# Attention of a hybrid encoder block: matmul pairs over halves of 64 array columns, values as the stationary side, probabilities normalised before they are split

## The chip, the cores and the metric

The kernel runs on one core of a Trainium2 chip. The metric is the time of one execution on the device in microseconds (us), as the median of several runs; lower is better. The engines are named as in the profile: PE is TensorE's matmuls and PEld its weight loads, DVE is VectorE, ACT is ScalarE, POOL is GpSimd, SP is SyncE, which here only issues DMAs.

## The reference

One encoder layer over 1024 tokens of width 1024, in float32. A combined projection gives queries, keys, values and gates of two groups of eight heads, 64 wide.

```python
h = jnp.einsum('bsd,de->bse', x, w_in[layer])
q_a, k_a, v_a, z_a, q_b, k_b, v_b, z_b = jnp.split(h, SPLIT_POINTS, axis=-1)
y_a = neighborhood_attention(q_a, k_a, v_a, rel_pos_bias[layer])   # heads of 64 split off
y_b = windowed_gqa_with_sink(rotary(q_b), rotary(k_b), v_b, sink_logits[layer])
mixed = jnp.concatenate([y_a * jax.nn.silu(z_a), y_b * jax.nn.silu(z_b)], axis=-1)
y = jnp.einsum('bse,ed->bsd', mixed, w_out[layer])
x = layer_norm(DEEPNORM_ALPHA * x + y, ln_gain[layer], ln_bias[layer])
```

Group A attends within a window of 8 x 16 in a grid of 16 rows and 64 columns, with a learned bias. Group B attends to keys at most 128 positions away; four query heads share one key and value head, and a learned sink logit stands in each softmax's sum. Both are softmax(scores) times values.

## The kernel before, in words

*Precision.* Every product is made from float16 halves: an operand is scaled and split into a high part and the remainder, and three of the four partial products are added up in PSUM (high x high, high x low, low x high).

*Stages.* First the values of all heads are projected (L487). Then the 21 projections of `ORDER` follow, each of 128 output columns: queries and keys of a pair of heads, or gates (z for group A, zb for group B). A projection has two halves of 512 tokens with 24 matmuls each (L380). The first `NPRO` = 6 stand ahead of the attention. The other 15 are the filler: `pump_to` puts their matmuls between those of the attention, so that projection `FILL[k]` is spread over the steps from `FILL_AT[k]` to `FILL_AT[k+1]`. After them, the first part of the output projection (`out_head`) is spread in the same way. `final` does the rest of the output projection (L1002), the residual and the layer norm.

*Attention.* There are 128 units, one for each group, pair of heads `p`, head `j` of the pair and block `t` of 128 queries. One step of the main loop (L1152) starts one unit, and issues the later stages of units before it. The order in which the program writes the instructions is the order on each engine:

- `stage_qk`: two matmuls of 256 or 384 keys (L797, L798), queries stationary, into one of four PSUM banks with the tag "s". Then VectorE adds bias or mask and takes the extremum of each row (L805).
- `stage_exp`: ScalarE's exponential with the row sum (L821), written back to the same bank.
- `stage_tr`, `LTT` steps later: the high part of the probabilities by ScalarE (L829), the low part by VectorE (L830), and a DMA that transposes both to `tr` (L833), issued by SP. The bank is free after that.
- `stage_pv`, once for four units (a quad), when the last of them is `LPP` steps and a few more behind: 33 matmuls (L856), with a transposed block of probabilities stationary and 64 columns of values moving. The result has queries on partitions.
- `stage_on`: VectorE multiplies by the reciprocal of the row sums (L862, L865).
- `stage_ot`, when both heads of the pair are done: four transposes through TensorE (L876), and VectorE's product with the gates (L879 for group B, L882 for group A).

Splits of projected queries and keys (L250 to L258, L298), of weights (L192 to L198), scans and scales of weights and the like are in queues, one for each engine; each step takes one or two from each, and `need` emits what a unit cannot do without, wherever it stands. `bank` hands out PSUM banks in turn: two for the projections ("pj"), four "s", two "t". Group A's values are gathered from DRAM by `gather_v`; the bias tiles are loaded `LD` = 7 steps ahead.

Of the kernel before, what the change touches and what calls it, by code (L numbers as in the profile page):

```python
# [35 lines left out]
FILL_AT = [0, 8, 17, 25, 33, 41, 49, 57, 66, 74, 81, 89, 97, 105, 112, 121, 123.5, 126, 128, 131, 136]  # L36
# [5 lines left out]
VA_STEP = (0, 1, 1)  # L42
# [7 lines left out]
WP = 256  # L50
BWIN = (0, 256, 640, 896)
# [4 lines left out]
def hybrid_block(ctx, tc, xT, x, wt, wv, wo, bias, sink, gain, lbias, cos, sin, bmask, out):  # L56
# [304 lines left out]
    def project(name):  # L361
        n = ORDER.index(name)
        w_split(2 * n + 2)
        for half in range(2):
            ps = new_group()
            for k in range(KT):
                if k % 4 == 0:
                    need(w_ops[2 * n + k // 4])
                h, l = parts[2 * n + k // 4]
                if n + 2 < NPRO and half == 0 and k == 4:  # L370
                    w_scan(2 * n + 4)
                if n + 2 < NPRO and half == 1 and k == 0:
                    w_scan(2 * n + 5)
                if half == 0 and k == 4:
                    w_split(2 * n + 3)
                if n + 2 < NPRO and half == 1 and k == 6:
                    w_scale(n + 2)
                for i, (a, b) in enumerate(((h, x16h), (h, x16l), (l, x16h))):
                    mv = b[half, k]
                    nc.tensor.matmul(ps, a[:, k % 4, :], mv,  # L380
                                     start=(k == 0 and i == 0), stop=(k == KT - 1 and i == 2))
# [370 lines left out]
    sns = [ap.tile([128, 388], F32, name=f"sn{i}", bufs=1) for i in range(2)]  # L752
# [5 lines left out]
    on = {}  # L758
# [18 lines left out]
    def stage_qk(u):  # L777
# [19 lines left out]
        nc.tensor.matmul(ps[:, :n], q, sl[0], start=True, stop=False)  # L797
        nc.tensor.matmul(ps[:, :n], q, sl[1], start=False, stop=True)  # L798
        s0 = sns[units.index(u) % 2]
# [11 lines left out]
    def stage_exp(u):  # L811
        n, _c = geom(u)
        m = n + 1 if u[0] == "b" else n
        sn, nm = st.pop((u, "sn")), st.pop((u, "nm"))
        pt = st.pop((u, "ps"))
        k = units.index(u) % 4
        if k == 0:
            st["sm"] = ap.tile([128, 4], F32, tag="sm", name="sm", bufs=4)
        sm = st["sm"]
        st[units.index(u) // 4, "sm"] = sm  # L820
        nc.scalar.activation(pt[:, :m], sn[:, :m], AF.Exp, bias=nm, scale=-1.0, accum_out=sm[:, k:k + 1])  # L821
        st[u, "p"] = pt

    def stage_tr(u):
        n, m = geom(u)
        pt = st.pop((u, "p"))
        hl = split[units.index(u) % NSPLIT]
        src = pt[:, :n].rearrange("p (k c) -> p k c", c=128)
        nc.scalar.activation(hl[:, :m, 0, :], src, AF.Copy, scale=PSCALE)  # L829
        nc.vector.scalar_tensor_tensor(hl[:, :m, 1, :], src, PSCALE, hl[:, :m, 0, :],  # L830
                                       op0=ALU.mult, op1=ALU.subtract)
# [8 lines left out]
    def stage_pv(q):  # L840
        ps = st[q, "o"] = bank("t")
        for m in range(4):
            u = units[4 * q + m]
            g, p, j, t = u
            tr = st.pop((u, "tr"))
            mms = []
            for i in range(geom(u)[1]):
                k = max(t - 1, 0) + i
                if g == "a":
                    v = [va[p][:, k, 128 * j + 64 * e:128 * j + 64 * e + 64] for e in range(2)]  # L850
                else:
                    v = [vb[:, k, p // 2, e, :] for e in range(2)]
                ph, pl = tr[:, 2 * i, :], tr[:, 2 * i + 1, :]
                mms += [(ph, v[0]), (ph, v[1]), (pl, v[0])]
            for i, (a, b_) in enumerate(mms):
                nc.tensor.matmul(ps[:, HD * m:HD * m + HD], a, b_, start=(i == 0), stop=(i == len(mms) - 1))  # L856

    def stage_on(q):
        g, p, j, h = quad(q)
        ps = st.pop((q, "o"))  # L860
        ri = ap.tile([128, 4], F32, tag="ri", name="ri", bufs=4)
        nc.vector.reciprocal(ri, st.pop((q, "sm")))  # L862
        if j == 0:
            on[g, p, h] = ap.tile([128, 4, 2, HD], F32, tag="on", name="on", bufs=2)
        nc.vector.tensor_mul(on[g, p, h][:, :, j, :], ps[:, :4 * HD].rearrange("p (m e) -> p m e", e=HD),  # L865
                             ri.unsqueeze(2).to_broadcast([128, 4, HD]))

    def stage_ot(q):
        g, p, j, h = quad(q)
        if j == 0:  # L870
            return
        need(*stk_ops.get(f"zb{p}" if g == "b" else f"z{p}", ()))
        ps = bank("t")
        o = on.pop((g, p, h))
        for i in range(4):
            nc.tensor.transpose(ps[:, 128 * i:128 * i + 128], o[:, i].rearrange("p h e -> p (h e)"), identf)  # L876
# [3 lines left out]
        else:  # L880
            z = zt[p].rearrange("p (r c) -> p c r", c=GW)[:, 32 * h:32 * h + 32, :]
            nc.vector.scalar_tensor_tensor(z, ps.rearrange("p (c r) -> p c r", r=ROWS), z_col(p), z,  # L882
# [56 lines left out]
    def wo_scale():  # L939
        need(*[wo_ops["s", n] for n in range(16)])  # L940
        ps = bank("t")
        nc.tensor.matmul(ps[:, :16], ones, wom.bitcast(BF16)[:, 1::2], start=True, stop=True)
# [46 lines left out]
    LO = LP + 4  # L989
    Q30 = LP + 3 + 4 * (len(units) // 4 - 2)  # L990
    NU = len(units)
    def out_mms(t, a, ps, es, c=(0, 512)):
        o, w = c
        ts, cs = slice(128 * t, 128 * t + 128), slice(o, o + w)
        ps = ps[:, o:o + w]
        for e in es:
# [4 lines left out]
            for i, (lh, rh) in enumerate(((mh[e], woh), (mh[e], wol), (ml[e], woh))):  # L1001
                nc.tensor.matmul(ps, lh[:, ts], rh[:, cs],  # L1002
                                 start=(e == EO[0] and i == 0), stop=(e == EO[-1] and i == 2))
# [4 lines left out]
    def out_head(ts, es, tag):  # L1008
# [6 lines left out]
        for e in es:  # L1015
            for t in ts:
                yield from out_mms(t, 0, obank[t, 0], [e])
# [134 lines left out]
    for i in range(-LD, NU + LO):  # L1152
# [43 lines left out]
        if m == 0 and 0 <= q - 1 < NU // 4:  # L1196
            stage_ot(q - 1)
# [8 lines left out]
        if 0 <= q < NU // 4:  # L1206
            g, p, j, h = quad(q)
            if g == "a" and p < 3 and (j, h, m) == VA_STEP:
                gather_v(p + 1)
        if m == 1 and 0 <= q < NU // 4:  # L1210
            stage_on(q)
# [83 lines left out]
```

## Time and profile before

| | us |
|---|---|
| median of 3 runs | 451.24 |
| lowest and highest | 451.11, 451.66 |
| the profiled execution's own time | 448.97 |
| its span, from the first to the last instruction | 447.2 |
| TensorE matmuls busy | 437.1 |
| VectorE busy | 349.0 |
| ScalarE busy | 309.9 |
| GpSimd busy | 212.0 |

The profile is of one execution. A group's row gives the line of the code, engine, operation, output and inputs, shape and count, then the busy time in us and the mean ns of one instruction, and then the engine's idle time just ahead of them with what ended it. A row of the timeline gives start and length in us. A matmul's length contains its passage through the array, so the distance between starts says what it costs the engine. A row of the table by windows gives the stretch, its length, and each engine's busy time with its number of instructions, then TensorE's granted clock, the share of the DMA engines and GB/s. In a row of waits stand who waited, at which line, for whom, us in total, times, and the longest.

### The profile page before, as it was taken

The numbers are of one execution on the slowest core, as the hardware profiler recorded it, in microseconds if no ns is written. First come the engines' busy times: TensorE is split into PE (matmuls) and PEld (weight loads), VectorE is DVE, ScalarE is ACT, GpSimd is POOL, SyncE is SP. The second block draws the span as 40 slices with busy tenths as digits, with TensorE's granted clock in tenths as the row PEclk, the third lists the DMA queues.
The fourth block names the chain that finished last, engine by engine and source line by source line (L and its number), as shares of the span: only waits on it lengthen the run. The fifth ranks groups of instructions, "written<-read, shape, count | busy, mean of one in ns | idle before, by whom it ended". The sixth has DMA issues, their size and how long they took to land.

```text
span 447.2 us, 9320 instructions
## 1 busy us (share of the span) xinstructions
PE 437.1 (98%) x3241; PEld 252.9 (57%) x3241; DVE 349.0 (78%) x840; ACT 309.9 (69%) x700; POOL 212.0 (47%) x219
## 2 busy tenths in 40 slices
PE   9999999999999999999999999999979999999995
PEld 8997754444445565555555655555536654444454
DVE  5978867438977898887898888888778847679944
ACT  5759789766599987877867887788777957012401
POOL 0110064637749559766424757565462404304740
PEclk9999999999999999999999999999999999999998
DMA  8921569980169999596986669569669598102711
GB/s 269 391 89 59 170 233 327 319 269 25 53 141 197 212 197 175 105 159 123 166 120 116 130 143 172 93 135 200 131 131 188 102 188 320 47 1 83 247 72 71
DMA packets 123984, 71.21 MB, mean 159 GB/s; under 512 B 96800, under 2 KB 105888, under 8 KB 123936
## 3 DMA queue, kind: packets, MB, share of 16 engines
q1 hardware_dynamic: 123792, 70.48, 65.8%
q8 instruction: 25, 0.41, 0.4%
q14 instruction: 23, 0.19, 0.2%
q10 hardware_dynamic: 144, 0.13, 0.1%
HBM read 41.23 MB, written 6.29 MB: 106 GB/s over the span
## 4 chain that ended last, share of the span: by engine, by line
PE 77%; DVE 10%; ACT 7%; issue 5%; DVEq 0%; ACTq 0%
PE ps_pj L380 36%; PE ps_s L1002 8%; PE ps_s L487 6%; PE ps_pj L1002 5%; PE ps_t L856 5%; PE ps_pj L487 3%; PE ps_t L487 3%; PE ps_t L1002 3%; PE ps_s L797 3%; PE ps_s L798 3%; ACT split L829 3%; ACT ps_s L821 2%; DVE split L830 2%; DVE qs L256 2%; DVE ks L256 1%
## 5 line engine op out<-in xcount | busy, mean ns | idle before, releaser
L380 PE MATMUL ps_pj<-xf,wh 128*128 128x512 f16 x672 | 202.1, 379 | 0.4 <-DVE ks L256 0.4
L380 PE MATMUL ps_pj<-xf,wl 128*128 128x512 f16 x336 | 127.3, 379 | 0.0
L380 PEld LDWEIGHTS <-wh 128*128 128x128 f16 x672 | 63.6, 98 | 61.6 <-DVE ks L256 1.2
L830 DVE SCALAR_TENSOR_TENSOR split<-ps_s,split 128x384 f16<-128x384 f32 (+1 forms) x128 | 66.9, 522 | 28.9 <-ACT split L829 27.5
L821 ACT ACTIVATE ps_s<-sn,nm 128x385 f32<-128x385 f32 (+3 forms) x128 | 71.0, 554 | 26.3 <-DVE nm L805 25.6
L1002 PEld LDWEIGHTS <-m 128*128 128x128 f16 x432 | 40.0, 98 | 41.6 <-DVE m L910 0.7
L829 ACT ACTIVATE split<-ps_s 128x384 f16<-128x384 f32 (+1 forms) x128 | 58.6, 458 | 2.4
L380 PEld LDWEIGHTS <-wl 128*128 128x128 f16 x336 | 32.8, 98 | 37.5
L197 POOL TENSOR_SCALAR wr<-wr,wsc 128x512 f32<-128x512 f32 x26 | 20.5, 789 | 67.7 <-ACT wh L192 61.2
L797 PE MATMUL ps_s<-ks,qs 128*128 128x384 f16 (+1 forms) x128 | 40.0, 313 | 2.9 <-DVE qs L256 2.9
L805 DVE CUSTOM_DVE_ANT_0 sn<-ps_s,bm,nsk 128x384 f32<-128x384 f32 (+1 forms) x64 | 40.7, 636 | 1.4 <-PE ps_s L798 1.2
L1002 PE MATMUL ps_s<-wo,m 128*128 128x512 f16 (+1 forms) x192 | 40.7, 366 | 0.2 <-DVE m L910 0.2
L798 PE MATMUL ps_s<-ks,qs 128*128 128x384 f16 (+1 forms) x128 | 40.0, 313 | 0.0
L805 DVE CUSTOM_DVE_ANT_0 sn<-ps_s,bias,sg 128x384 f32<-128x384 f32 (+1 forms) x64 | 37.0, 578 | 2.6 <-PE ps_s L798 2.0
L856 PEld LDWEIGHTS <-tr 128*128 128x128 f16 x1056 | 35.2, 98 | 2.5
L198 POOL TENSOR_TENSOR wl<-wr,wh 128x512 f16<-128x512 f32 x26 | 32.7, 1256 | 2.2
L298 POOL COPY ks<-ks 64x512 f16<-64x512 f16 x40 | 26.1, 661 | 10.3 <-DVE ks L256 3.4
L197 POOL TENSOR_SCALAR ws<-ws,wsc 128x512 f32<-128x512 f32 x16 | 11.1, 691 | 33.9 <-ACT wh L192 30.1
L1002 PE MATMUL ps_pj<-wo,m 128*128 128x512 f16 (+1 forms) x144 | 26.5, 326 | 0.0
L1101 POOL TENSOR_TENSOR xr<-xr,gb 128x512 f32<-128x512 f32 x7 | 9.8, 1396 | 32.5 <-ACT xr L1098 32.5
L821 ACT ACTIVATION_READ_ACCUMULATOR ps_s<-sn,nm 128x1 f32 x128 | 24.4, 191 | 0.0
L797 PEld LDWEIGHTS <-qs 128*128 128x128 f16 x128 | 12.5, 98 | 18.4 <-DVE qs L256 3.4
(187 smaller groups left out, 800.2 us busy)
## 6 DMA issues: line engine op xcount, KB each, us to landing
ws<-in_wt SPq DMA_DIRECT2D x15, 512.0 KB, 5.8
wr<-in_wt SPq DMA_DIRECT2D x26, 256.0 KB, 3.8
wor<-in_wo SPq DMA_DIRECT2D x22, 256.0 KB, 3.5
xr<-in_x SPq DMA_DIRECT2D x8, 512.0 KB, 9.0
out<-xr SPq DMA_DIRECT2D x15, 256.0 KB, 2.1
bias<-in_bias SPq DMA_DIRECT2D x8, 448.0 KB, 3.9
wvraw<-in_wv SPq DMA_DIRECT2D x9, 320.0 KB, 5.9
xraw<-in_xT SPq DMA_DIRECT2D x11, 256.0 KB, 4.5
```

The source lines that it names most:

```text
L197: nc.gpsimd.tensor_scalar(raw, raw, scale, 1.0, op0=ALU.mult, op1=ALU.mult)
L198: nc.gpsimd.tensor_sub(l, raw, h)
L380: nc.tensor.matmul(ps, a[:, k % 4, :], mv, start=(k == 0 and i == 0), stop=(k == KT - 1 and i == 2))
L487: nc.tensor.matmul(ps[:, :320], lh[:, ts], rh[:, cs], start=(k == ko[0] and i == 0), stop=(k == ko[-1] and i == 2))
L797: nc.tensor.matmul(ps[:, :n], q, sl[0], start=True, stop=False)
L798: nc.tensor.matmul(ps[:, :n], q, sl[1], start=False, stop=True)
L805: nc.vector.tensor_tensor_reduce(sn[:, :n], ps[:, :n], bias_t, sg[:, c:c + 1], init, op0=ALU.add, op1=ALU.min, accum_out=nm)
L821: nc.scalar.activation(pt[:, :m], sn[:, :m], AF.Exp, bias=nm, scale=-1.0, accum_out=sm[:, k:k + 1])
L829: nc.scalar.activation(hl[:, :m, 0, :], src, AF.Copy, scale=PSCALE)
L830: nc.vector.scalar_tensor_tensor(hl[:, :m, 1, :], src, PSCALE, hl[:, :m, 0, :], op0=ALU.mult, op1=ALU.subtract)
L856: nc.tensor.matmul(ps[:, HD * m:HD * m + HD], a, b_, start=(i == 0), stop=(i == len(mms) - 1))
L1002: nc.tensor.matmul(ps, lh[:, ts], rh[:, cs], start=(e == EO[0] and i == 0), stop=(e == EO[-1] and i == 2))
```

## The change: what it does

Matmuls of the attention stage are issued twice, each over 64 of the 128 columns of the stationary operand, with outputs on partitions 0 to 63 and 64 to 127 (`HALVES`). This holds for the scores, for the 15 projections of the filler, for the output heads and for a small scale product that stands among them, which also moves from a "t" to an "s" bank.

In the value products the sides are swapped. The 64 columns of values are stationary and the 128 transposed probabilities move; the head j=0 writes the lower half of the partitions and j=1 the upper. The result has head dimensions on partitions, as the gate product needs it. `stage_on`, `stage_ot` and the transposes through TensorE are gone, and `stage_gate` keeps the gate product, for group A with the other one of its operands read in strides.

For this, the units alternate between the heads of a pair after every second block. The reciprocal of the row sums is taken for two units at a time at the start of a step (`stage_ri`) and goes in as the scale of the split. The split stands two steps behind the exponential (`LTT` = 2, before 1), and there are four score buffers `sns` in place of two. z2 is projected earlier, ahead of k1, and the steps of some later projections move. The loop ends three steps earlier after the last unit.

```diff
-LTT, LPP, BP, BH, BR, ND, NA, NX, F1 = 1, 6, 2, 9, 5, 1, 1, 6, 0.2
+LTT, LPP, BH, ND, NA, NX, F1 = 2, 6, 9, 1, 1, 6, 0.2
-ORDER = ["zb0", "z0", "zb1", "kb", "qb0", "z1", "qb1", "zb2", "qb2", "k0", "qb3", "zb3", "q0", "k1", "q1",
-         "k2", "q2", "z2", "k3", "q3", "z3"]
+ORDER = ["zb0", "z0", "zb1", "kb", "qb0", "z1", "qb1", "zb2", "qb2", "k0", "qb3", "zb3", "q0", "z2", "k1",
+         "q1", "k2", "q2", "k3", "q3", "z3"]
-FILL_AT = [0, 8, 17, 25, 33, 41, 49, 57, 66, 74, 81, 89, 97, 105, 112, 121, 123.5, 126, 128, 131, 136]
+FILL_AT = [0, 8, 17, 25, 33, 41, 49, 57, 64.5, 71.5, 78, 85.5, 93, 101, 109, 121, 123.5, 126, 128, 131, 136]
-VA_STEP = (0, 1, 1)
+VA_STEP = (1, 2)
+HALVES = (slice(0, 64), slice(64, 128))
...
-                    nc.tensor.matmul(ps, a[:, k % 4, :], mv,
-                                     start=(k == 0 and i == 0), stop=(k == KT - 1 and i == 2))
+                    for c in HALVES if n >= NPRO else (slice(0, 128),):
+                        nc.tensor.matmul(ps[c], a[:, k % 4, c], mv,
+                                         start=(k == 0 and i == 0), stop=(k == KT - 1 and i == 2))
...
-                for j in range(2):
-                    for i in range(8):
-                        us.append((g, p, j, i))
+                for i in range(0, 8, 2):
+                    for j in range(2):
+                        us.extend((g, p, j, t) for t in (i, i + 1))
...
-    sns = [ap.tile([128, 388], F32, name=f"sn{i}", bufs=1) for i in range(2)]
+    sns = [ap.tile([128, 388], F32, name=f"sn{i}", bufs=1) for i in range(4)]
...
-        nc.tensor.matmul(ps[:, :n], q, sl[0], start=True, stop=False)
-        nc.tensor.matmul(ps[:, :n], q, sl[1], start=False, stop=True)
-        s0 = sns[units.index(u) % 2]
+        for i in range(2):
+            for c in HALVES:
+                nc.tensor.matmul(ps[c, :n], q[:, c], sl[i], start=(i == 0), stop=(i == 1))
+        s0 = sns[units.index(u) % 4]
...
+    def stage_ri(i):
+        ri = ap.tile([128, 2], F32, tag="ri", name="ri", bufs=4)
+        nc.vector.reciprocal(ri, st["sm"])
+        nc.vector.tensor_scalar_mul(ri, ri, PSCALE)
+        for k in range(2):
+            st[units[i - 2 + k], "ri"] = ri[:, k:k + 1]
...
-        nc.scalar.activation(hl[:, :m, 0, :], src, AF.Copy, scale=PSCALE)
-        nc.vector.scalar_tensor_tensor(hl[:, :m, 1, :], src, PSCALE, hl[:, :m, 0, :],
+        nc.scalar.activation(hl[:, :m, 0, :], src, AF.Copy, scale=ri)
+        nc.vector.scalar_tensor_tensor(hl[:, :m, 1, :], src, ri, hl[:, :m, 0, :],
                                        op0=ALU.mult, op1=ALU.subtract)
...
     def stage_pv(q):
-        ps = st[q, "o"] = bank("t")
-        for m in range(4):
-            u = units[4 * q + m]
-            g, p, j, t = u
-            tr = st.pop((u, "tr"))
-            mms = []
-            for i in range(geom(u)[1]):
+        g, p, _j, h = quad(q)
+        if q % 2 == 0:
+            st["o"] = bank("t")
+        ps = st["o"]
+        for m in range(2):
+            us = units[4 * q + m], units[4 * q + 2 + m]
+            t = us[0][3]
+            trs = [st.pop((u, "tr")) for u in us]
+            n = geom(us[0])[1]
+            for i in range(n):
                 k = max(t - 1, 0) + i
-                if g == "a":
-                    v = [va[p][:, k, 128 * j + 64 * e:128 * j + 64 * e + 64] for e in range(2)]
-                else:
-                    v = [vb[:, k, p // 2, e, :] for e in range(2)]
-                ph, pl = tr[:, 2 * i, :], tr[:, 2 * i + 1, :]
-                mms += [(ph, v[0]), (ph, v[1]), (pl, v[0])]
-            for i, (a, b_) in enumerate(mms):
-                nc.tensor.matmul(ps[:, HD * m:HD * m + HD], a, b_, start=(i == 0), stop=(i == len(mms) - 1))
...
+                for e, w in ((0, 0), (1, 0), (0, 1)):
+                    for j, c in enumerate(HALVES):
+                        if g == "a":
+                            v = va[p][:, k, 128 * j + 64 * e:128 * j + 64 * e + 64]
+                        else:
+                            v = vb[:, k, p // 2, e, :]
+                        nc.tensor.matmul(ps[c, 128 * (t % 4):128 * (t % 4) + 128], v, trs[j][:, 2 * i + w, :],
+                                         start=(i + e + w == 0), stop=(i == n - 1 and w == 1))
...
-    def stage_on(q):
...
-    def stage_ot(q):
...
+    def stage_gate(q):
...
-        for i in range(4):
-            nc.tensor.transpose(ps[:, 128 * i:128 * i + 128], o[:, i].rearrange("p h e -> p (h e)"), identf)
...
-            z = zt[p].rearrange("p (r c) -> p c r", c=GW)[:, 32 * h:32 * h + 32, :]
-            nc.vector.scalar_tensor_tensor(z, ps.rearrange("p (c r) -> p c r", r=ROWS), z_col(p), z,
+            z = zt[p].rearrange("p (r c) -> p r c", c=GW)[:, :, 32 * h:32 * h + 32]
+            nc.vector.scalar_tensor_tensor(z, ps.rearrange("p (c r) -> p r c", r=ROWS), z_col(p), z,
                                            op0=ALU.mult, op1=ALU.mult)
...
-        ps = bank("t")
-        nc.tensor.matmul(ps[:, :16], ones, wom.bitcast(BF16)[:, 1::2], start=True, stop=True)
+        ps = bank("s")
+        for c in HALVES:
+            nc.tensor.matmul(ps[c, :16], ones[:, c], wom.bitcast(BF16)[:, 1::2], start=True, stop=True)
...
-    LO = LP + 4
+    LO = LP + 1
...
-                yield from out_mms(t, 0, obank[t, 0], [e])
+                yield from out_mms(t, 0, obank[t, 0], [e], rows=HALVES)
...
+        if i % 2 == 0 and 2 <= i <= NU:
+            stage_ri(i)
```

More of the change, by code (lines that the diff above doesn't have):

```diff
@@ L816, in stage_exp @@
         k = units.index(u) % 4
-        if k == 0:
-            st["sm"] = ap.tile([128, 4], F32, tag="sm", name="sm", bufs=4)
+        if k % 2 == 0:
+            st["sm"] = ap.tile([128, 2], F32, tag="sm", name="sm", bufs=4)
         sm = st["sm"]
-        st[units.index(u) // 4, "sm"] = sm
-        nc.scalar.activation(pt[:, :m], sn[:, :m], AF.Exp, bias=nm, scale=-1.0, accum_out=sm[:, k:k + 1])
+        nc.scalar.activation(pt[:, :m], sn[:, :m], AF.Exp, bias=nm, scale=-1.0, accum_out=sm[:, k % 2:k % 2 + 1])
         st[u, "p"] = pt
+    def stage_ri(i):
[4 more added lines that the diff above has]
+            st[units[i - 2 + k], "ri"] = ri[:, k:k + 1]
     def stage_tr(u):
         n, m = geom(u)
+        ri = st.pop((u, "ri"))
         pt = st.pop((u, "p"))
@@ L858, in stage_on @@
-    def stage_on(q):
[L859 to L866, printed above, removed]
-    def stage_ot(q):
-        g, p, j, h = quad(q)
-        if j == 0:
+        g, p, _j, h = quad(q)
@@ L1001, in out_mms @@
             for i, (lh, rh) in enumerate(((mh[e], woh), (mh[e], wol), (ml[e], woh))):
-                nc.tensor.matmul(ps, lh[:, ts], rh[:, cs],
-                                 start=(e == EO[0] and i == 0), stop=(e == EO[-1] and i == 2))
+                for d in rows:
+                    nc.tensor.matmul(ps[d, cs], lh[:, 128 * t + d.start:128 * t + d.stop], rh[:, cs],
+                                     start=(e == EO[0] and i == 0), stop=(e == EO[-1] and i == 2))
                 yield
```

17 lines of the change are left out of this document (7 added, 10 removed).

## The prediction

> **What bounds the kernel now.** I read the busy shares of the page first, then the chain that ended last, then single matmuls in the timeline, because the page warns that a busy TensorE is not one at its peak.
>
> ```profile
> span 447.2 us, 9320 instructions
> PE 437.1 (98%) x3241; PEld 252.9 (57%) x3241; DVE 349.0 (78%) x840; ACT 309.9 (69%) x700; POOL 212.0 (47%) x219
> PE 77%; DVE 10%; ACT 7%; issue 5%; DVEq 0%; ACTq 0%
> ```
>
> TensorE has 437.1 of 447.2 us and 77% of the chain. The timeline of one attention step shows whether those 98% are real, from the distances between starts.
>
> ```profile
> 300.10 0.59 PE L380 MATMUL ps_pj<-xf,wh 128*128 128x512 f16 x2
> 300.53 0.38 PE L380 MATMUL ps_pj<-xf,wl 128*128 128x512 f16 x1
> 300.75 0.33 PE L797 MATMUL ps_s<-ks,qs 128*128 128x384 f16 x1
> 300.91 0.33 PE L798 MATMUL ps_s<-ks,qs 128*128 128x384 f16 x1
> 301.07 1.13 PE L856 MATMUL ps_t<-va,tr 128*128 128x64 f16 x33
> 302.04 0.59 PE L380 MATMUL ps_pj<-xf,wh 128*128 128x512 f16 x2
> ...
> 308.52 0.60 PE L876 MATMUL ps_t<-identf,on 128*128 128x128 f32 x4
> 308.95 1.13 PE L856 MATMUL ps_t<-va,tr 128*128 128x64 f16 x33
> ```
>
> A 512-wide projection matmul takes (300.53 - 300.10)/2 = 0.215 us of the engine, a 384-wide score matmul 0.16. The 33 value products of a quad take 302.04 - 301.07 = 0.97, or 0.0294 each; four transposes take 308.95 - 308.52 = 0.43, or 0.1075 each. Nothing lies between them: each starts where the one before stops streaming. Steps are as long as TensorE's work in them, and the only long hole shows in the waits and in the rows of the score matmul:
>
> ```profile
> PE ps_s L797 <- DVE qs L256: 2.9, 1, 2.9
> 333.85 0.28 PE L797 MATMUL ps_s<-ks,qs 128*128 128x256 f16 x1 [2.94 <-DVE qs L256]
> L797 PE MATMUL ps_s<-ks,qs x128: 269/326/326, 121.3 to 358.0; 128*128 128x384 f16 x96, 128*128 128x256 f16 x32
> ```
>
> The 128 steps run from 121.3 to 358.0, so one is (358.0 - 121.3)/127 = 1.86 us. The hole at 333.85 is unit 112, the first of the last pair of group A: its q3 is projected from step 105 to 112, and the wait is for the split of that q. The kernel is bound by TensorE, and what an edit there saves or costs, it saves or costs in time.
>
> **The change, part by part.**
>
> *Transposes.* L876 goes: the swapped products come out transposed. Of 32 quads every second one transposed four blocks: 16 x 0.43 = 6.9 us saved, all on the path.
>
> *Value products.* There are 1056 as before, but now 128 wide, and two of them share the array. Today they take 32 x 0.97 = 31.0 us. The end of the trace shows 128-wide streams, in the timeline and in the groups:
>
> ```profile
> 437.33 2.73 PE L1002 MATMUL ps_pj<-wo,m 128*128 128x128 f16 x46
> L1002 PE MATMUL ps_pj<-wo,m 128*128 128x128 f16 x48 | 2.8, 219 | 0.0
> ```
>
> One of these lasts 0.219 us, so 46 of them in 2.73 start (2.73 - 0.219)/45 = 0.056 us apart. If the two halves run together, 528 pairs take 528 x 0.056 = 29.5 us at the least; if each instruction needs the 0.0294 us that is the shortest distance seen, 528 x 0.0587 = 31.0. I take the second: no change.
>
> *Projection, scores and output heads in halves.* 15 x 48 = 720 projection matmuls, 256 score matmuls and 60 of the output heads become pairs: 1036 second halves. Nothing in the trace runs two matmuls at once. From below a second half costs nothing (the same stream enters the array, and a gain is excluded, since the stream is no shorter). From above it costs the whole stream again: 720 x 0.215, and the other 316 at about 0.16, 155 + 51 = 206 us. Between them lies one issue distance, 1036 x 0.0294 = 30.5 us. I take nothing, since the rows nearest to it are today's weight loads, which go in beside the stream:
>
> ```profile
> 300.32 0.10 PEld L380 LDWEIGHTS <-wl 128*128 128x128 f16 x1
> 300.53 0.10 PEld L797 LDWEIGHTS <-qs 128*128 128x128 f16 x1
> ```
>
> Each lasts 0.10 us and starts while a 0.215 us stream runs; a pair has two such slots. The Trainium skill, TensorE: Matmul & The Clock Gate, section Measured speedup vs the span model, has three column tiles at 2.38 times and about 4 ns for each further tile. By that figure 1036 second halves would be an estimated 4.1 us and the forecast 446.5. No run here shows it yet.
>
> *Order of projections.* z2 moves ahead of k1, and q3 is now projected from step 101 to 109, needed at 112: three steps, 5.6 us, where there were none. The 2.9 us hole goes. What is late next is q1 (71.5 to 78, needed at 80): two steps, 3.7 us, against two ACT and two VectorE splits in sequence, (2 x 0.585 + 2 x 0.69) = 2.5 us by these rows:
>
> ```profile
> L250 ACT ACTIVATE qs<-ps_pj 64x512 f16<-64x512 f32 x16 | 9.4, 585 | 5.5 <-DVE qs L256 5.5
> L256 DVE SCALAR_TENSOR_TENSOR qs<-ps_pj,qs 64x512 f16<-64x512 f32 x16 | 11.0, 688 | 1.1 <-ACT qs L250 0.7
> ```
>
> It fits. Head j=1 of a pair is now needed two steps after j=0, not eight; both are split from one projection, so this costs at most those same 2.5 us a pair, and I take none. The bias loads of the two heads come two steps apart in place of eight, still seven steps ahead; the gather of the next v moves one step, eleven steps before its use. Both stay hidden by these steps.
>
> *VectorE and ScalarE.* These are the cover, so I add them up over the steady stretch, which holds 118 of the units and 27 quads.
>
> ```profile
> 121.20:345.00 223.80, 220.47 (x1920) 124.81 (x1918) 187.39 (x507) 183.39 (x465) 131.93 (x143) 1.00 0.80 151
> L865 DVE TENSOR_TENSOR on<-ps_t,ri 128x256 f32<-128x256 f32 x27 | 11.5, 424 | 0.9
> L862 DVE RECIPROCAL ri<-sm 128x4 f32<-128x4 f32 x32 | 5.4, 168 | 0.0
> L235 DVE TENSOR_SCALAR zc<-zi 128x1 f32<-128x1 f32 x1 | 0.2, 153 | 0.0
> L237 DVE TENSOR_SCALAR zc<-inv,zi 128x1 f32<-128x1 f32 x2 | 0.3, 202 | 0.0
> L314 ACT ACTIVATE rp_raw<-ps_pj 128x512 f32<-128x512 f32 x10 | 5.9, 593 | 6.2 <-PE ps_pj L380 6.2
> L344 ACT ACTIVATE z<-ps_pj,invt 128x512 f32<-128x512 f32 x10 | 6.8, 682 | 5.6 <-PE ps_pj L380 3.8 <-POOL rp_raw L316 1.8
> ```
>
> VectorE loses the normalising multiply (11.5) and 27 reciprocals (27 x 0.168 = 4.5). It gains, for each of 59 unit pairs, a reciprocal and a scaling (0.168 + 0.153), 18.9 us; and the low-part split reads its scale from a column, not a constant, which by L237 against L235 is 0.049 us, 118 times, 5.8. That is 187.4 + 8.7 = 196.1. ScalarE's high part gets a column scale too: by L344 against L314, 0.089 x 118 = 10.5, so 193.9. Group A's gate changes which operand is read in strides; its price lies between the two gates' rows, so it saves between nothing and 7 x 0.42 = 2.9, and I count none:
>
> ```profile
> L882 DVE SCALAR_TENSOR_TENSOR z<-ps_t,zc,z 128x512 f32<-128x512 f32 x8 | 9.3, 1168 | 7.4 <-PE ps_t L876 7.4
> L879 DVE SCALAR_TENSOR_TENSOR z<-ps_t,zc,z 128x512 f32<-128x512 f32 x8 | 6.0, 747 | 0.0
> ```
>
> TensorE's part of this stretch shrinks to 223.8 - 13 x 0.43 - 2.9 = 215.3. VectorE then is at 91% of it and ScalarE at 90%, where they were at 84% and 82%. VectorE may stand idle 19.2 us in place of 36.4. Most of what it idles now is this:
>
> ```profile
> DVE split L830 <- ACT split L829: 25.9, 47, 1.4
> ACT ps_s L821 <- DVE nm L805: 23.3, 37, 2.1
> ```
>
> LTT = 2 puts a whole step between the exponential and the split, which takes the first wait away. The reciprocal brings a new one: at every second step VectorE waits for the exponential of the unit before, with the score sum of the next unit queued behind it. One step's queue lies between, so I expect it short; four score buffers in place of two help. A score bank is now freed by the split in step i-2 and not i-3 for the score of step i, so TensorE can run two steps ahead of VectorE, no longer three (the output scale takes one such bank once, at step 55). I charge 1.0 us for the thinner cover; the ends are 0 and, if VectorE's idle time does not shrink at all, 196.1 + 36.4 - 215.3 = 17.2.
>
> *The transposing DMAs* start one step later against an unchanged LPP = 6: the last one of a quad is issued in step 4q+5 and used in step 4q+9, so three whole steps, 5.6 us, are left; on SP each now stands behind the loads of one step more.
>
> ```profile
> DMA to landing us min/median/max: 2.4/3.2/5.8
> ```
>
> The median landing, 3.2 us, fits; the longest, 5.8, does not. I charge nothing and keep this as a rival. The loop ends three steps sooner after the last unit (LO is LP + 1, not LP + 4). Output heads that were spread over those steps now stand behind them, the same work in the same order for TensorE, so I count nothing.
>
> **Sum.** 448.97 (the profiled execution's own time, span 447.2 and 1.8 around it) - 6.9 - 2.9 + 1.0 = 440.2 us. The median of the runs, 451.24, is 2.27 above that execution; with the same distance the forecast is 442.4 us.
>
> **The rivals.**
>
> *Weight loads of the value products show.* A pair streams for only 0.056 us and needs two loads of 64 columns. The row nearest to a load that shows is L876: 0.1075 us from start to start for a 128-wide stream with f32 weights, twice the 0.056 of f16. If a pair of products takes that, 528 x (0.1075 - 0.0587) = 25.8 us come on top: 448.97 - 9.8 + 25.8 = 465.0, as a median 467.2. It decides from 0.0587 + 9.8/528 = 0.077 us a pair; above this the kernel is slower. Against it: L856's loads today overlap each other, 33 of them in 0.97 us at 0.10 us each. The rule for it is the Trainium skill's, TensorEngine Tiling (Array Packing), Restrictions: column tiling disables fast weight load; the same page's Key Properties let different tiles load and multiply in parallel, which speaks for the forecast. No row here decides between them.
>
> *Halves queue.* If each second half costs one issue distance, 30.5 us: 448.97 - 9.8 + 30.5 = 469.7, as a median 471.9. If the halves run one after the other, 206 us: about 647. For it there is only that no row shows concurrency; against it that the stream is common.
>
> *VectorE and ScalarE take over.* If VectorE's idle time falls from 36.4 to only 24, the stretch takes 220.1, 4.8 over TensorE's 215.3, and the median is 448.97 - 9.8 + 4.8 + 2.27 = 446.2. It costs all of the gain at 29, and at 36.4 gives 458.6.
>
> *Transposes land late.* If a third of 32 quads wait half a step, 11 x 0.93 = 10.2 us: 448.97 - 9.8 + 10.2 + 2.27 = 451.6.
>
> **How the numbers follow.** Forecast, 437 to 446: 0.52. VectorE and ScalarE: 0.16 (0.11 faster, 0.02 same, 0.03 slower). Weight loads: 0.13, slower. An issue distance per half: 0.06; halves in sequence: 0.03; both slower. Late transposes: 0.10 (0.03 faster, 0.02 same, 0.05 slower). That is faster 0.66, same 0.04, slower 0.30, where same means within 0.2%, 0.9 us, about what can be told apart here. The lower bound is 448.97 - 6.9 - 2.9 - 1.5 = 437.7, with value pairs 0.056 apart and a median as low as the profiled execution; one execution and the median differ by 2.27 already, so I set it 1.7 lower, at 436. The upper end, 460, takes in the second and the last rival and the lower half of the weight loads; left out are 0.07 of these, 0.06 and 0.03.
>
> **What would show it.** In the changed profile, starts of projection pairs 0.215 us apart and of value pairs 0.056 to 0.059; no transposes; no wait at L797 for a split of q3; VectorE near 91% of the stretch with the wait for ScalarE's split nearly gone and a shorter one at the reciprocal. I am wrong if value pairs are over 0.077 apart, projection pairs over 0.225, or if TensorE shows holes before value products or scores.

## The result, and the profile after

The changed kernel takes 473.69 us (median of 4 runs, 472.35 to 475.0) against 451.18 of the kernel before: a ratio of 1.0507, with a 95% interval of 1.0457 to 1.0556. It is 22.5 us slower where 8.8 us less were forecast, and it lies outside the stated range. The profiled execution took 474.88 us, 25.9 more than that of before. All times below are medians of fast executions: one execution of no_ri_ltt1, 2486.52 us at a granted clock of 0.17, is left out.

The page, first its span and busy times:

```profile
span 473.2 us, 11261 instructions
PE 440.9 (93%) x4214; PEld 283.9 (60%) x4214; DVE 372.0 (79%) x904; ACT 319.4 (68%) x700; POOL 208.5 (44%) x219
```

TensorE's share fell from 98% to 93%, and VectorE was busy 23 us longer. The table by windows follows for the stretch of the 128 steps, from the first score matmul to the last. The first row is of the kernel before, the second of the changed one; the columns are those named in the section on the profile before.

```profile
121.30:358.00 236.70, 233.37 (x2043) 132.53 (x2042) 198.76 (x538) 194.39 (x494) 136.39 (x147) 1.00 0.79 149
```

```profile
121.90:384.10 262.20, 237.75 (x2984) 162.79 (x2984) 223.47 (x604) 203.32 (x492) 135.84 (x147) 0.99 0.73 134
```

All of the loss is here: 262.2 - 236.7 = 25.5 us. A step takes 2.06 us, not 1.86. The timeline of after, TensorE alone, shows where:

```profile
300.39 0.63 PE L382 MATMUL ps_pj<-xf,wh 128*64 128x512 f16 x4
300.83 0.41 PE L382 MATMUL ps_pj<-xf,wl 128*64 128x512 f16 x2
...
302.02 0.52 PE L800 MATMUL ps_s<-ks,qs 128*64 128x384 f16 x4
302.34 0.62 PE L382 MATMUL ps_pj<-xf,wh 128*64 128x512 f16 x4
...
305.75 0.41 PE L382 MATMUL ps_pj<-xf,wh 128*64 128x512 f16 x2
307.47 0.52 PE L800 MATMUL ps_s<-ks,qs 128*64 128x384 f16 x4 [1.32 <-DVE split L839]
307.80 1.03 PE L867 MATMUL ps_t<-tr,va 128*64 128x128 f16 x30
308.63 0.41 PE L382 MATMUL ps_pj<-xf,wh 128*64 128x512 f16 x2
```

The matmuls do what was forecast. Two projection pairs take 300.83 - 300.39 = 0.44 us, 0.22 a pair; two score pairs take 0.32; fifteen pairs of value products take 308.63 - 307.80 = 0.83, 0.055 a pair. The time is lost ahead of the score matmul at 307.47: TensorE waits for VectorE's split (L839) of the unit four before, which frees the score bank. The waits of after say the same, and who holds up that split:

```profile
PE ps_s L800 <- DVE split L839: 19.4, 29, 2.4
DVE split L839 <- ACT split L838: 22.2, 56, 1.5
DVE ri L827 <- ACT ps_s L822: 6.3, 21, 0.8
ACT split L838 <- issue: 12.6, 9, 1.6
PE ps_t L867 <- DMA tr<-split: 2.6, 3, 1.4
```

A matmul's row runs on past its stream, so these waits understate the holes. From the distances between starts, less 0.216, 0.163, 0.109 or 0.056 us for a single matmul or a pair of its width, I add up 34.4 us of holes over the attention, 29.3 of them ahead of scores; before there were 4.2 us. Such a count is good to about 1 us.

The groups of after that are new or longer, behind the two splits of before with their wait:

```profile
L830 DVE SCALAR_TENSOR_TENSOR split<-ps_s,split 128x384 f16<-128x384 f32 (+1 forms) x128 | 66.9, 522 | 28.9 <-ACT split L829 27.5 <-POOL wl L198 0.4
L829 ACT ACTIVATE split<-ps_s 128x384 f16<-128x384 f32 (+1 forms) x128 | 58.6, 458 | 2.4
```

```profile
L839 DVE SCALAR_TENSOR_TENSOR split<-ps_s,ri,split 128x384 f16<-128x384 f32 (+1 forms) x128 | 74.6, 583 | 24.6 <-ACT split L838 22.2
L828 DVE TENSOR_SCALAR ri<-ri 128x2 f32<-128x2 f32 x64 | 25.8, 403 | 2.2
L838 ACT ACTIVATE split<-ps_s,ri 128x384 f16<-128x384 f32 (+1 forms) x128 | 69.7, 545 | 31.8 <-issue 12.6
```

L828 is the scaling of two reciprocals by 2^14. It should take as long as the reciprocal beside it and takes 0.403 us on average. One line of the timeline of after, with its neighbours on VectorE, GpSimd and ScalarE, shows what it does in that time:

```profile
301.80 1.16 POOL L970 TENSOR_TENSOR wo<-wor,wo 128x512 f16<-128x512 f32 x1
301.95 0.17 DVE L827 RECIPROCAL ri<-sm 128x2 f32<-128x2 f32 x1
...
302.15 0.83 DVE L828 TENSOR_SCALAR ri<-ri 128x2 f32<-128x2 f32 x1
...
302.89 0.60 DVE L807 CUSTOM_DVE_ANT_0 sn<-ps_s,bias,sg 128x384 f32<-128x384 f32 x1
...
303.06 0.58 ACT L838 ACTIVATE split<-ps_s,ri 128x384 f16<-128x384 f32 x1 [1.14 <-issue]
...
303.67 0.62 DVE L839 SCALAR_TENSOR_TENSOR split<-ps_s,ri,split 128x384 f16<-128x384 f32 x1 [0.17 <-ACT split L838]
```

GpSimd's instruction ends at 301.80 + 1.16 = 302.96, L828 at 302.98. Of the 64, the 30 that began while GpSimd was idle took 0.169 to 0.171 us. Of the other 34, 32 ended 0.022 to 0.029 us after the instruction that GpSimd was running, up to 1.17 us after their start. Behind L828 stand the score sum of the step (L807) on VectorE and the split (L838) on ScalarE. The split idles 1.14 us; the profile names no releaser ("issue"), but it starts 0.08 us after the end of L828, whose result it reads. Behind that stands the low split, and behind that TensorE.

The Trainium skill, SBUF — State Buffer, section Who interferes with whom, has this as a rule: VectorE and GpSimd share one pair of SBUF ports; a VectorE instruction in a two-port mode contends for it, and one with two SBUF inputs does so with a GpSimd instruction that reads SBUF; whoever comes second is blocked for the other's whole instruction. The rows agree in that L828 ends just behind GpSimd's instruction; in which mode L828 runs, no row shows.

### The profile page after: what moved, and what is told of

Same layout as the page of the kernel before. It is cut to its first block, busy times and chain, and to the rows that moved or that the text cites. A ratio compares the mean times of both kernels' runs of the same rounds, so it can differ in the third digit from the quotient of the medians.

```text
span 473.2 us, 11261 instructions
## 1 busy us (share of the span) xinstructions
PE 440.9 (93%) x4214; PEld 283.9 (60%) x4214; DVE 372.0 (79%) x904; ACT 319.4 (68%) x700; POOL 208.5 (44%) x219
## 5 line engine op out<-in xcount | busy, mean ns | idle before, releaser
L382 PE MATMUL ps_pj<-xf,wh 128*64 128x512 f16 (+1 forms) x1152 | 210.9, 381 | 0.0
L382 PE MATMUL ps_pj<-xf,wl 128*64 128x512 f16 (+1 forms) x576 | 134.3, 381 | 0.0
L382 PEld LDWEIGHTS <-wh 128*64 128x64 f16 (+1 forms) x1152 | 82.4, 108 | 47.1 <-issue 0.6
L839 DVE SCALAR_TENSOR_TENSOR split<-ps_s,ri,split 128x384 f16<-128x384 f32 (+1 forms) x128 | 74.6, 583 | 24.6 <-ACT split L838 22.2
L838 ACT ACTIVATE split<-ps_s,ri 128x384 f16<-128x384 f32 (+1 forms) x128 | 69.7, 545 | 31.8 <-issue 12.6
L800 PE MATMUL ps_s<-ks,qs 128*64 128x384 f16 (+1 forms) x512 | 63.3, 318 | 21.9 <-DVE split L839 19.4
L1002 PEld LDWEIGHTS <-m 128*128 128x128 f16 (+1 forms) x492 | 42.6, 101 | 39.9 <-issue 1.4
L800 PEld LDWEIGHTS <-qs 128*64 128x64 f16 x512 | 33.8, 110 | 52.1 <-issue 31.2
L382 PEld LDWEIGHTS <-wl 128*64 128x64 f16 (+1 forms) x576 | 42.4, 109 | 28.1 <-issue 0.4
L807 DVE CUSTOM_DVE_ANT_0 sn<-ps_s,bm,nsk 128x384 f32<-128x384 f32 (+1 forms) x64 | 40.7, 636 | 1.3 <-PE ps_s L800 1.0
L1002 PE MATMUL ps_s<-wo,m 128*128 128x512 f16 (+2 forms) x228 | 40.5, 368 | 0.4 <-DVE split L839 0.4
L807 DVE CUSTOM_DVE_ANT_0 sn<-ps_s,bias,sg 128x384 f32<-128x384 f32 (+1 forms) x64 | 37.0, 578 | 2.5 <-PE ps_s L800 1.0
L828 DVE TENSOR_SCALAR ri<-ri 128x2 f32<-128x2 f32 x64 | 25.8, 403 | 2.2
```

Source lines behind the costliest of these rows:

```text
L382: nc.tensor.matmul(ps[c], a[:, k % 4, c], mv, start=(k == 0 and i == 0), stop=(k == KT - 1 and i == 2))
L800: nc.tensor.matmul(ps[c, :n], q[:, c], sl[i], start=(i == 0), stop=(i == 1))
L807: nc.vector.tensor_tensor_reduce(sn[:, :n], ps[:, :n], bias_t, sg[:, c:c + 1], init, op0=ALU.add, op1=ALU.min, accum_out=nm)
L828: nc.vector.tensor_scalar_mul(ri, ri, PSCALE)
L838: nc.scalar.activation(hl[:, :m, 0, :], src, AF.Copy, scale=ri)
L839: nc.vector.scalar_tensor_tensor(hl[:, :m, 1, :], src, ri, hl[:, :m, 0, :], op0=ALU.mult, op1=ALU.subtract)
```

## The experiments

Theory 1 was that the split, moved two steps behind, holds the score banks; theory 2 that VectorE and ScalarE are too slow for the step; theory 3 that the halves slow TensorE.

**Free the score bank at once (p_sbuf).**

```diff
-        nc.scalar.activation(pt[:, :m], sn[:, :m], AF.Exp, bias=nm, scale=-1.0, accum_out=sm[:, k % 2:k % 2 + 1])
-        st[u, "p"] = pt
+        nc.scalar.activation(sn[:, :m], sn[:, :m], AF.Exp, bias=nm, scale=-1.0, accum_out=sm[:, k % 2:k % 2 + 1])
+        st[u, "p"] = sn
```

> The exponential writes its probabilities over the scores in SBUF, not into the PSUM bank of the scores; the bank is then free as soon as VectorE has read it, in the unit's own step, and no longer two steps later. Theory 1 (TensorE's work is as forecast; the time is lost because the split, two steps late, holds the score bank, 29 us of holes ahead of the score matmuls): those holes go, 440 to 450 us. Theory 2 (VectorE and ScalarE are simply too slow for the step, whatever they hold): the holes move to the value products, 462 to 475 us. Theory 3 (the halves themselves slow TensorE): no change, 472 to 476 us.

Measured: 491.03 us, worse than any forecast (ratio to before 1.0899, 1.0852 to 1.0946). Its waits and its low split:

```profile
PE ps_t L867 <- DMA tr<-split: 22.7, 19, 3.4
L839 DVE SCALAR_TENSOR_TENSOR split<-sn,ri,split x128: 473/619/1610, 126.7 to 406.6; 128x384 f16<-128x384 f32 x96, 128x256 f16<-128x256 f32 x32
```

The wait for score banks is gone and the holes moved on to the value products, as theory 2 has it. But the edit did two things more, neither of them foreseen. The split now has both inputs in SBUF, and where it took 0.62 us at most it takes up to 1.61. And the granted clock over the steps was 0.95, where the change had 0.99:

```profile
211.40 1.12 PE L867 MATMUL ps_t<-tr,vb 128*64 128x128 f16 x17 [2.91 <-DMA tr<-split]
212.25 1.11 PE L382 MATMUL ps_pj<-xf,wh 128*64 128x512 f16 x4
213.11 0.69 PE L382 MATMUL ps_pj<-xf,wl 128*64 128x512 f16 x2
```

```profile
212.30:217.20 4.90, 4.90 (x31) 2.75 (x28) 3.89 (x11) 4.84 (x12) 2.35 (x3) 0.50 0.58 110
```

Here two projection pairs take 213.11 - 212.25 = 0.86 us, 0.43 a pair and not 0.22, at a clock of 0.50. So the run shows that freeing the banks does not bring the time back while the split is late, but not what the banks alone cost. Against theory 1 as the main cause speak no_ri and before_ltt2 below: there the split also stands two steps behind, and the one is no slower than the kernel before, the other by 0.7 us.

**Another form of the scaling (ri_mul2).** `psc` is a constant tile that holds 2^14.

```diff
-        nc.vector.tensor_scalar_mul(ri, ri, PSCALE)
+        nc.vector.tensor_mul(ri, ri, psc)
```

> The reciprocal is multiplied by a constant tile in a two-input instruction in place of a constant in a one-input one. In the changed kernel the one-input form takes 0.169 us while GpSimd is idle, but ends 0.025 us after GpSimd's running instruction when there is one. Theory 1: VectorE's scaling falls from 25.8 to about 11 us in all, the split is freed earlier at every second step, and 5 to 13 us of the holes go: 460 to 469 us. Theory 2 gives the same. Theory 3: 472 to 476 us. If the instruction still waits for GpSimd, the form is not the cause.

Measured: 473.72 us, no change, and outside the ranges of theories 1 and 2, since the edit did not take the wait away:

```profile
L830 DVE TENSOR_TENSOR ri<-ri,psc 128x2 f32<-128x2 f32 x62 | 24.3, 392 | 2.1
```

The form with two SBUF inputs waits as the one-input form did. So the one-input form was not the cause by itself, and the run doesn't tell theory 3 from the others.

**No normalisation (no_ri).**

```diff
-        if i % 2 == 0 and 2 <= i <= NU:
-            stage_ri(i)
...
-        nc.scalar.activation(hl[:, :m, 0, :], src, AF.Copy, scale=ri)
-        nc.vector.scalar_tensor_tensor(hl[:, :m, 1, :], src, ri, hl[:, :m, 0, :],
+        nc.scalar.activation(hl[:, :m, 0, :], src, AF.Copy, scale=PSCALE)
+        nc.vector.scalar_tensor_tensor(hl[:, :m, 1, :], src, PSCALE, hl[:, :m, 0, :],
```

> Leaves out the normalisation: no reciprocal, no scaling, and the split takes a constant scale again, still two steps late. VectorE loses 35 us and some 6 of the column scale, ScalarE 11 us. Theory 1: the split then runs early enough most of the time, 443 to 453 us, with some holes left from the two steps. Theory 2: 441 to 446 us, near the forecast. Theory 3: 470 to 474 us.

Measured: 449.3 us, just under the kernel before (0.9969, 0.9949 to 0.9989). That is in theory 1's range and 3.3 us above theory 2's, so neither has it whole: the two-step split still costs something here, and no_ri_ltt1 below says how much. Halves, swapped products and unit order are all still there, so theory 3 is out: what stands in VectorE's and ScalarE's normalisation is worth 473.7 - 449.3 = 24.4 us, more than the whole loss. About 11.6 us of holes stay, somewhat over half of them ahead of value products and the others ahead of scores.

**Projections at full width (full_proj).**

```diff
-                    for c in HALVES if n >= NPRO else (slice(0, 128),):
+                    for c in (slice(0, 128),):
```

> Undoes the halves for the 15 projections alone, so that 128-column and 64-column matmuls alternate two or three times a step. Theories 1 and 2: the projections gain nothing, since pairs stream in 0.216 us as the single matmul did; what the alternation costs is unknown, from nothing (472 to 476 us) to the 0.16 us that a matmul lasts beyond its stream, at each of some 4 changes a step, part of it inside the holes (up to 500 us). Theory 3: 450 to 460 us.

Measured: 477.27 us, 3.6 more than the change. The timeline of this run:

```profile
201.19 0.38 PE L382 MATMUL ps_pj<-xf,wl 128*128 128x512 f16 x1
201.50 0.52 PE L800 MATMUL ps_s<-ks,qs 128*64 128x384 f16 x4
201.95 0.60 PE L382 MATMUL ps_pj<-xf,wh 128*128 128x512 f16 x2
```

From the last full matmul to the first half there are 0.31 us, where its stream takes 0.216: a hole of 0.09. Back again it is 0.45 us for two score pairs of 0.163 each: 0.12. Holes of this kind stand at each of some 240 changes; that is an estimated 24 us at 0.1 each, and as the run is only 3.6 us longer, most of them stand in place of holes that were there anyway. The projection in halves avoids them; what that is worth in a kernel without the other holes, no run here shows. The Trainium skill, TensorEngine Tiling (Array Packing), Key Properties, says that changing the tiling mode drains TensorE, without a price; about 0.1 us is what it costs here.

For the second round the question was what in the normalisation costs: A, the two instructions on VectorE; B, ScalarE's split waiting for VectorE's reciprocal; C, the column scale.

**Compute the reciprocals, don't use them (ri_unused).** The constant scales of no_ri, with `stage_ri` kept.

> Leaves out the normalisation: the reciprocal and its scaling are still computed, but both halves of the split take a constant scale, so that ScalarE no longer waits for VectorE's reciprocal and no column scale is read. Theory A (the two instructions added on VectorE, with their wait for GpSimd, are the loss): 464 to 473 us. Theory B (the split on ScalarE waiting for VectorE's reciprocal closes a loop between the two): 449 to 457 us. Theory C (the column scale makes both splits slower): 455 to 463 us.

Measured: 466.2 us. The instructions alone, with nobody waiting for their result, cost 466.2 - 449.3 = 16.9 us. That is A, in its range. The delay goes through the score sum that stands behind them on VectorE, for which ScalarE's exponential waits, first without them (no_ri) and then with them:

```profile
ACT ps_s L822 <- DVE nm L807: 34.4, 47, 2.5
ACT ps_s L822 <- DVE nm L807: 53.6, 63, 2.4
```

**Use a column, compute nothing (col_const).** `psc` of ri_mul2 is the scale of both splits; `stage_ri` is not called.

> Leaves out the normalisation: no reciprocal and no scaling, but both halves of the split read their scale from a constant column. Theories A and B: 449 to 454 us, as without any normalisation. Theory C: 458 to 468 us.

Measured: 454.6 us, 5.3 more than with a constant: C is real and small, just past A's and B's upper end.

**Drop the 2^14 (no_pscale).**

```diff
-PSCALE = 2.0 ** 14
+PSCALE = 1.0
...
-        nc.vector.tensor_scalar_mul(ri, ri, PSCALE)
```

> The probabilities are no longer multiplied by 2^14, so the scaling behind the reciprocal goes, with the 25.8 us that it takes and waits on VectorE; the reciprocal, its wait for the exponential and the column scale stay. Theory A: 454 to 461 us. Theory B: 462 to 470 us, for the split then waits for a shorter time, but it waits. Theory C: 466 to 473 us.

Measured: 455.4 us (1.0088, 1.0057 to 1.0118), in A's range. One instruction of two elements a partition, 64 times, was worth 18.3 us.

**One step, not two (no_ri_ltt1).** no_ri with `LTT = 1`.

> Leaves out the normalisation as before (no reciprocal, constant scale) and puts the split one step behind the exponential, not two. If the 11.6 us of holes that were left without the normalisation come from the two steps (transposes that land late, score banks held), they go: 440 to 445 us, which is the forecast's sum. If not: 447 to 450 us.

Measured: 445.28 us, the median of the three executions that count (0.9874, 0.9844 to 0.9903), just past the first range. The second step costs 449.3 - 445.28 = 4.0 us. About 8 us of holes stay, most of them ahead of value products, where TensorE waits for transposes:

```profile
PE ps_t L866 <- DMA tr<-split: 4.5, 7, 2.1
PE ps_s L800 <- DVE split L838: 1.5, 3, 0.6
```

The third round asked how the scaling costs so much.

**Its place, without its wait (no_pscale_twice).** no_pscale, with a second reciprocal into a tile of its own just ahead of the first.

> Without the 2^14 (455.4 us), and with each reciprocal computed a second time into a tile that nobody reads: 64 instructions more on VectorE of 0.16 us, 10.4 us in all, of a form that did not wait for GpSimd in any trace so far. They stand where the scaling stood. If the scaling cost its own 0.17 us and the place in VectorE's order, this brings most of its 18.3 us back: 466 to 473 us. If it cost the wait for GpSimd's instruction, on top of 0.17 us: 457 to 464 us.

Measured: 458.62 us, in the second range. The reciprocal in the scaling's place does not wait:

```profile
L829 DVE RECIPROCAL ri<-sm x64: 135/145/158, 125.9 to 369.6; 128x2 f32<-128x2 f32 x64
```

64 instructions of about 0.15 us in that place cost 3.2 us; the scaling cost 18.3. The difference, 15 us, is what L828 waited for GpSimd: 25.8 - 64 x 0.169 = 15.0 us.

**The reciprocal behind the score sum (no_pscale_late).** no_pscale, with the call of `stage_ri` moved below `stage_qk(u)` in the same step.

> Without the 2^14 (455.4 us), and with the reciprocal behind the score sum of its step, not ahead of it. VectorE no longer waits 6.2 us for the exponential there, and the scores of the step are summed sooner; ScalarE's split waits longer for the reciprocal (10.2 us now). If VectorE's order is the bound: 450 to 454 us. If ScalarE's start into the step is: 456 to 462 us.

Measured: 467.0 us, 11.6 slower, and beyond the second range. Its waits:

```profile
ACT split L837 <- DVE ri L827: 28.5, 41, 1.7
DVE split L838 <- ACT split L837: 53.1, 81, 1.5
```

Not one instruction more: only that ScalarE gets its scale some 0.7 us later at every second step. A delay ahead of ScalarE's split goes from there to VectorE's split and to TensorE. So theory B is a real mechanism too. In the change as it stands it is worth little, though: of the 473.7 - 466.2 = 7.5 us that ri_unused is faster, the column scale accounts for 5.3.

**The order of projections alone (before_order).** `ORDER` and `FILL_AT` of the change in the kernel before.

> The kernel before with the change's order of projections and their times alone: z2 ahead of k1, q3 ready at step 109 in place of 112. By the prediction the one hole ahead of the score matmuls, 2.9 us by the waits, goes and nothing takes its place: 447.8 to 448.8 us. If the denser filler makes the steps from 57 to 109 wait elsewhere: 450 to 453 us.

Measured: 449.29 us (0.9963, 0.995 to 0.9976), 1.8 us off and between the two ranges. The hole of 2.9 us at q3 is gone, and smaller ones stand ahead of the scores: its longest waits of this kind are

```profile
PE ps_s L797 <- DVE split L830: 0.8, 2, 0.5
PE ps_s L797 <- DVE qs L256: 0.6, 1, 0.6
```

By the medians this is the best of the versions here that compute the whole block. But the gain is not the hole's own 2.9 us. The profiled executions of both, at granted clocks of 0.997 and 0.998, have spans of 447.2 us before and 447.3 here: what the hole gave back, smaller ones took. The medians differ together with the clock: all five executions here had a clock of 0.997 or 0.998 (449.01 to 449.74 us), while of the 15 of before beside them only four had (448.84 to 450.2), and the other eleven had 0.990 to 0.995 (450.82 to 451.63). Why the clock is steadier with the new order, and whether the hole had to do with it, no trace here shows.

**The second step in the kernel before (before_ltt2).** `LTT = 2`, nothing else.

> The kernel before with the split two steps behind the exponential, nothing else. If the later split costs by holding score banks and by late transposes whatever the kernel: 453 to 458 us, with holes ahead of score matmuls and value products. If it costs only where VectorE and ScalarE have no room left: 450 to 452 us.

Measured: 451.86 us (1.0026, 1.0009 to 1.0042), in the second range. Two steps cost next to nothing in the kernel before, where VectorE is not behind.

**The same scaling, one element at a time (ri_two_cols).** The whole change, 2^14 included.

```diff
-        nc.vector.tensor_scalar_mul(ri, ri, PSCALE)
+        for k in range(2):
+            nc.vector.tensor_scalar_mul(ri[:, k:k + 1], ri[:, k:k + 1], PSCALE)
```

> The changed kernel with the scaling of two reciprocals written as two instructions of one element a partition each, the result the same. If an instruction of one element does not wait for GpSimd, 64 x 0.31 = 20 us without waits take the place of 25.8 us with them, at the place where 10.4 us of waitless instructions cost 3.2 us: 459 to 464 us. If it waits like the form of two elements, the first of each two waits and the second follows: 474 to 480 us, and the wait belongs to the operation and its operands, not to the number of elements.

Measured: 462.43 us, in the first range and 11.3 less than the change, with twice as many instructions for the scaling:

```profile
L829 DVE TENSOR_SCALAR ri<-ri x128: 142/149/156, 125.8 to 376.6; 128x1 f32<-128x1 f32 x128
```

None of the 128 waits, though GpSimd was running at the start of 70 of them. With no_pscale_twice this settles it: not the value, the place or the number of instructions, but the wait for GpSimd. The 7.0 us that are left over no_pscale are the price of 128 instructions that do not wait.

Read from the forecast up, the loss is a ladder of medians: 442.4 forecast; 445.3 without normalisation and with one step; 449.3 with two; 454.6 with the column scale; 455.4 with the reciprocals; 473.7 with the scaling.

## Why the prediction was wrong, point by point

*TensorE's part was right.* Projection and score pairs cost what the single matmuls did, value pairs 0.055 us, and the transposes' 6.9 us were saved: from no_ri's 236.5 us of steps I take its 11.6 of holes, 224.9, and from before's 236.7 its 4.2, 232.5, which leaves 7.6 us less work, give or take the 1 us of such counts. Two rivals were priced near the result, weight loads (467.2) and halves that queue (471.9), and neither is what happened. A total near a rival's price is no evidence for it; the distances between starts rule both out. The weight loads of 64 columns take 0.110 us each, where those of 128 took 0.098, and stay hidden even in pairs that stream for 0.055 us. So the rule of the Trainium skill, TensorEngine Tiling (Array Packing), Restrictions, that column tiling disables fast weight load, which stood behind one rival, costs no time here.

*The step that failed is the sum for VectorE, and in it the price of one term.* For the scaling it took L235, 0.153 us. That row is of one element a partition, from ahead of the attention. L828 took 0.403, so the term was 9.8 us for 64 and is 25.8, of which 15.0 us are the wait for GpSimd. The trace of before had shown such waits, in two groups that I left aside because they stand outside the attention:

```profile
L687 DVE COPY vb<-vt x8: 226/228/1070, 67.3 to 81.5; 128x256 f16<-128x256 f16 x8
L1064 DVE SCALAR_TENSOR_TENSOR nmr<-mv,rstd x8: 147/160/1208, 404.4 to 441.8; 128x1 f32<-128x1 f32 x8
```

In L1064 one and the same tiny instruction has a median of 0.160 us and a longest of 1.208: three of the eight end with an instruction of GpSimd's, 0.015 to 0.017 us behind it. The longest of L687 ends 0.085 us behind one. L1064 has two inputs in SBUF, and L687 is a copy of one; neither is the form of L828, so they were a warning and not a price. The other terms held: the column scale is 0.061 us on VectorE (583 against 522; 0.049 forecast) and 0.087 on ScalarE (545 against 458; 0.089 forecast), and group A's gate became cheaper by 0.42 us, the end of its range that I did not count. VectorE's added work over the 128 steps is 223.5 - 198.8 = 24.7 us, where 8.7 was summed for 118 units.

*The second failure is the charge of 1.0 us for a thinner cover.* The rival that VectorE and ScalarE take over had the mechanism, with 458.6 as its worst end: all of VectorE's idle time stays. So it was. VectorE idled 236.7 - 198.8 = 37.9 us in the steps before and 262.2 - 223.5 = 38.7 after. The stretch grew by the added work, 24.7 us, and by 0.8 us of idle time, which makes its 25.5. I had taken this idle time for slack that LTT = 2 would free; the wait for ScalarE's split did shrink only from 27.5 to 22.2 us, and the reciprocal's 6.3 came in its place. VectorE and ScalarE wait for each other in a ring, and work or waiting added in the ring adds to the step, though VectorE's busy share is only 223.5 / 262.2 = 85%. That it is this ring which keeps the idle time is read from the waits and from no_pscale_late; no run takes the ring apart.

*Smaller steps.* Late transposes: 2.6 us of waits in the change, about 6 us of holes where the normalisation is left out; a rival, not the cause. The q3 hole: its removal alone brought nothing between executions of one clock, as smaller holes took its place; the 2.9 us that the sum took for it were not there. ScalarE's added work was near the sum (203.3 - 194.4 = 8.9 us, 10.5 forecast), and its share told nothing: no_pscale_late lost 11.6 us with the same work.

## What to carry to other kernels

An instruction is priced from a row with the same operands and the same neighbours, and from its longest next to its median: a tiny VectorE instruction whose longest is seven times its median is waiting for something, and GpSimd is the first to look at. Where two engines hand work to each other every step, their idle time isn't free for new work, and an instruction that stands ahead of both sides of the exchange can cost its whole wait, as here 15 us of 15. Work that is saved on the bound engine shows only if the engines that feed it have room, so take the new work off these first, one instruction at a time, and read the ladder.

## What the runs showed of the hardware

- VectorE's instruction on 128x2 float32 in SBUF waited for GpSimd's running instruction with one input and a constant (0.403 us mean, 0.169 alone) and with two inputs (0.392); a reciprocal of the same size (0.162) and a scaling of 128x1 (0.149, 128 of 128) did not. The low split did not with its source in PSUM (longest 0.620 us), and did with its source in SBUF (longest 1.610). One element a partition waited too where both inputs were in SBUF (L1064, longest 1.208).
- Two matmuls of 64 columns each took the time of one of 128 columns: 0.216 us at 512 wide, 0.163 at 384, 0.055 at 128. A change between 64 and 128 columns left a hole of about 0.1 us.
- The granted clock was 0.50 from 212.3 to 217.2 us of p_sbuf, behind a hole of 2.91 us, and projection pairs started 0.43 us apart, not 0.216. Behind the hole of 2.94 us in the profiled execution of the kernel before it stayed 1.00.
